# Modulation chunks 0 to 2 in four column groups a step, chunk 3 summed by VectorE during the down projections of a hybrid transformer block

## The chip, the cores and the metric

The kernel runs on one core of a Trainium2 chip. The metric is the device time of one execution in microseconds; the time before is the median of 3 runs.

## The reference

One block of a diffusion transformer works on 256 latent tokens and 256 context tokens of width 2048. A vector `c` gives a modulation of six chunks of 2048 numbers. Two of them (shift and scale of the first norm) are needed for latents and context, the other four for the latents alone: the gate of the mixer, shift and scale of the second norm, the gate of the feed-forward network. In the kernel these four are the chunks 0, 1, 2 and 3.

```python
m_lat = jnp.split((jax.nn.silu(c) @ ada_w[i] + ada_b[i])[:, None, :], N_MOD, axis=-1)
...
a_lat = _modulate(h_lat, norm1_g[i], m_lat[0], m_lat[1]) @ w_in[i]
...
mix_l = jnp.concatenate([hyena_l, _retention_out(r_l, g_l),
                         _s5_out(y5_l, u_l, ...)], axis=-1) @ w_out[i]
...
h_lat = h_lat + m_lat[2] * mix_l
h_lat = h_lat + m_lat[5] * _conv_ffn(_modulate(h_lat, norm2_g[i], m_lat[3], m_lat[4]), ...)
...
return _rmsnorm(h_lat, norm_f)
```

The mixer has three parts: a Hyena convolution by Fourier transforms, a retention of 8 heads with decays in both directions, and an S5 state space scan. The feed-forward network is an up projection to twice 5632 features, a 3 by 3 convolution of one half, a gelu, the product with the other half and a down projection to 2048.

## The kernel before

Features lie on partitions, tokens along the free dimension. All weights come from HBM in blocks of 256 rows by 512 columns (512 KB). `split_w` loads a block by SP's DMA queue into a page of the ring "raw", ScalarE casts it to the high part (L454), VectorE takes the difference as the low part (L456), and `prod` makes three products of each pair (high by high, high by low, low by high: L461 to L463). `feat_block` has 24 products of 256 columns for one block. The products sum in two of the four PSUM banks "mm" per group of 512 features; small work uses three banks "sm", the modulation one bank "ad".

The large products follow each other: the S5 input while norm 1's modulation arrives, the keys, the values in two halves, the gate in two halves and the queries, the three Hyena projections, the output projection, then the feed-forward network in six groups of up and down projections. Between their blocks, tasks emit a piece of other work: the S5 chain, the retention, the Hyena chain, and `t_ada`, the modulation of chunks 0 to 3. A task's rate says how many of its steps are emitted per block: `RK` and `RV` in the keys and values, `RG` in gate and queries, `RH` in the Hyena projections, `RW` in the output projection, `RF` in the up projections. A scheduler of the language then puts each engine's instructions in order by their priority (the order of emission, with the weights' loads and casts moved ahead) and by the times at which it reckons that they can start. On the chip each engine takes its instructions in that order.

A chunk of the modulation is a vector of 2048 times a matrix of 2048 by 2048. `ada_matmul` makes it on TensorE, with 32 columns as weights (`cs`) and the matrix moving, 128 rows a step. The 2048 columns are four quarters `q` of 512, and quarter `q` is written to PSUM partitions 32q to 32q + 31, a column group of its own. A step is half of that, one page of 512 KB with two quarters:

```python
raw = [load_a(I["ada25"][c, kt, half]) for half in range(2)]
for half in (1, 0):
    for e in range(2):
        ...
    if (kt, half) != (KT - 1, 0):
        yield
```

The operands are 32-bit, and the trace has two records for each of these products. `ada_vector` instead adds each page, times its row's element of `cs`, to a page on VectorE (L428, L430), and sums over partitions by products with ones (L435). `ADV` lists the chunks that go this way: 1 and 2. `ada_store` transposes the sums (L397) into `ada_cols`. Pages come from the ring "ada", whose size after the S5 input is the first number of `RN`.

In `down`, each group's sums go straight to the residual, four instructions of 256 elements per 512 features (L1419):

```python
V.scalar_tensor_tensor(h_of(mt), at(m), ada_cols[:, 3, mt:mt + 1], h_of(mt), ALU.mult, ALU.add)
```

So chunk 3 is needed at the first down projection. In `retention`, the scores of the two heads of a pair are made one head after the other (L1158), each followed by its own decay and product with the values.

Of the kernel before, what the change touches and what calls it, by code (L numbers as in the profile page):

```python
# [16 lines left out]
P = 128  # L17
# [39 lines left out]
def _lay(i):  # L57
    """The inputs as the kernel reads them: slices, transposes and constants of the shapes."""
# [84 lines left out]
    # constants of the shapes  # L143
# [24 lines left out]
RN=[2,3,3,3];SA=40000;SF=30000;R0=10;R1=1;R2=1;RS=4;RK=2;RV=3;RG=.8;RH=.8;RW=.75;RF=.8;RT=1.2;RR=3;RY=.75;PR=500;ADV=[1,2];ORD=[0,1,2,3];RP=1.5;RQ=20;KS=5;PW=800;AR=[6,8,8,8,7,5,5,5];ZE=[1,3];VE=[0,1,3];UE=[1,3]  # L168
class _Pages:
    """Tags of fixed sizes in the slot pool, taken and given back in the order of the program."""  # L170
# [12 lines left out]
class _Ring:  # L183
    """Tags taken in turn."""
# [9 lines left out]
class _Task:  # L194
    """Work that is emitted piece by piece between the blocks of the large products."""
# [23 lines left out]
def tile_dit(ctx: ExitStack, tc: tile.TileContext, I, out: bass.AP, dbg=None):  # L219
# [14 lines left out]
    @contextmanager  # L234
    def stream(name, start):
        """Instructions whose order of priority starts at -start and goes on from use to use."""
        n = counts.get(name, 0)
        with tc.high_priority(offset=tc.cur_priority + start - n):
            before = tc.cur_priority
            yield  # L240
            counts[name] = n + tc.cur_priority - before
# [4 lines left out]
    def resize(kind, n):  # L246
        """A ring of n pages of 4 KB."""
        tags = ring[kind].tags
        while len(tags) < n:
            tags.append(pages.take(4))  # L250
        while len(tags) > n:
            pages.give(tags.pop())
# [53 lines left out]
    def sum_squares(ps, sq, first, last):  # L306
        """Sums over the partitions and parts of sq [P, n, w], a token on each partition."""
# [6 lines left out]
    def inv_rms(ps, n, w):  # L314
        """1/sqrt(sum/n + eps) of w tokens' sums, on all partitions."""
# [76 lines left out]
    def ada_store(c, ps):  # L392
        """Four rows of 512 columns to their places."""
# [10 lines left out]
    def ada_matmul(c):  # L404
        """2048 of the modulation's columns for the latents, as products of TensorE."""
        ps = ada_bank()
        for kt in range(KT):
            raw = [load_a(I["ada25"][c, kt, half]) for half in range(2)]
            for half in (1, 0):
                for e in range(2):  # L410
                    q = 2 * half + e
                    T.matmul(ps[32 * q:32 * q + 32, :], cs[:, kt, :], raw[half][:, e, :],  # L412
                             start=(kt == 0), stop=(kt == KT - 1), skip_group_check=True)
                if (kt, half) != (KT - 1, 0):
                    yield
# [3 lines left out]
    def ada_vector(c):  # L419
        """The same, summed over the rows' tiles by VectorE and over partitions by TensorE."""  # L420
        ps = ada_bank()
        for half in range(2):
            tag = pages.take(4)
            acc = slot(tag, [P, 2, 512])
            for kt in range(KT):
# [5 lines left out]
                if kt < KT - 1:  # L431
                    yield
            for e in range(2):
# [4 lines left out]
            if half == 0:  # L438
                yield
# [3 lines left out]
    def ada25():  # L443
        """The other four chunks of the modulation (2048 columns each), for the latents."""
# [14 lines left out]
    def prod(ps, a, b, first, last):  # L459
        """ps += a.T @ b with a = (high, low), b = (high, low)."""  # L460
# [12 lines left out]
    def feat_block(src, k0, at, mv, first, last):  # L473
        """256 rows of the weights into 512 features' sums: a bank's first start clears it for both."""
# [15 lines left out]
    hyk = [dram.tile([P, 4, 512], F32, name=f"hyk{o}") for o in range(2)]  # L490

    def sin_reduced(out_ap, x, w, k):
        """sin of x (SBUF [n, w]) with the argument reduced to [-pi, pi]; x is overwritten."""
# [8 lines left out]
    def hyena_filters():  # L502
# [36 lines left out]
        for o in range(2):  # L539
            # even and odd parts of the filter's lags  # L540
# [31 lines left out]
            for ft in (2, 3, 0, 1):  # L572
# [7 lines left out]
                if ft == 2:  # L580
                    # the first row is frequency 256, of the even part
# [10 lines left out]
    s5l = const.tile([P, 4, 2, 32], F32, name="s5l")  # L592
    s5 = {}
    # real parts and -/+ imaginary parts of lambda_bar to the powers 4, 8, 16 and one more
# [29 lines left out]
    def s5_prepare():  # L624
# [33 lines left out]
        # (lambda_bar - 1) / lambda  # L658
# [16 lines left out]
        # block-diagonal output matrices for the products within a chunk  # L675
# [3 lines left out]
        for qt in range(4):  # L679
            # the powers of lambda_bar times the input matrix  # L680
# [42 lines left out]
            # the products within a chunk by distance, then as a matrix of tokens by tokens  # L723
# [28 lines left out]
    # ======================= norm 1 and the S5 input, as the modulation arrives =======================  # L752
# [84 lines left out]
    # ======================= S5 =======================  # L837
# [3 lines left out]
    def s5_scan_input(v, quarter, held):  # L841
        """The chunks' additions to the states: of the context into v, of the latents into held."""
# [15 lines left out]
    def s5_add(v, dst, src, step, n, k):  # L858
        """v at dst, dst + step .. += lambda_bar^(4 * 2^k) * v at src, src + step .., n of them."""
# [23 lines left out]
    def s5_sum(v):  # L883
        """The state after 64 chunks from nothing, at 63."""
# [6 lines left out]
    def s5_scan(v):  # L891
        """From the state at 0 and the chunks' additions at 1..63, the states before all chunks."""
# [38 lines left out]
    def s5_chain():  # L931
# [26 lines left out]
        for hb in range(2):  # L958
# [21 lines left out]
            # in channels by tokens, where the context's part of u4 was  # L980
# [34 lines left out]
    # ======================= retention: keys and values =======================  # L1015
# [459 lines left out]
```

## Time and profile before

| | |
|---|---|
| median of 3 runs | 1506.35 us (1502.78 to 1508.24) |
| profiled execution, span from first to last instruction | 1506.4 us |
| TensorE busy (products) | 1459.1 us, 97% |
| VectorE busy | 1040.6 us, 69% |
| ScalarE busy | 658.0 us, 44% |
| DMA engines' time in packets | 65.4% of the span |
| read from HBM | 312.62 MB |

The profile is of one execution, of its own time: its span, 1506.4 us, lies between the lowest and the highest of the runs, and no other time of it is given. PE is TensorE, PEld its weight loads, DVE VectorE, ACT ScalarE, SP the engine whose queue starts the DMA transfers. A busy PE is not a PE at its peak, as its products overlap in the pipeline; distances between the starts of products are the better measure.

### The profile page before, as it was taken

To read this page: it belongs to the slowest core of one execution; us is meant where nothing else is said; L and a number is where in the kernel's file an instruction comes from. 1 tells how busy PE (TensorE), PEld (TensorE's weight loads), DVE (VectorE), ACT (ScalarE), POOL (GpSimd) and SP (SyncE) were. 2 spreads that over 40 slices of the span, in tenths; PEclk is the share of its full clock that TensorE was granted. 3 is DMA by queue.
4 is the path that set the end of the run, shared out by engine and by line. 5 is a ranking of instruction groups with operands and counts; after the bars stand their busy time and mean duration, and the time that the engine had idled before them with its cause. 6 is when DMAs were issued, how large, how long until landed. Compare 5 with 4: busy or idle time off the path is not lost.

```text
span 1506.4 us, 27320 instructions
## 1 busy us (share of the span) xinstructions
PE 1459.1 (97%) x11180; PEld 1314.7 (87%) x11180; DVE 1040.6 (69%) x1772; ACT 658.0 (44%) x974; POOL 10.9 (1%) x9
## 2 busy tenths in 40 slices
PE   6998999999999999999999999999999999999997
PEld 3566687678888987788899999999999999999997
DVE  6579519897869887653777665775667577657756
ACT  6337741213576433232554443443444344434434
POOL 0000000000000000000000000000000000000000
PEclk9999999999999999999999999999999999999998
DMA  9788635568877887677465666556665666656562
GB/s 352 260 313 291 229 101 197 183 194 278 281 252 253 299 303 261 219 226 251 145 182 183 185 182 184 185 177 192 183 183 182 182 183 183 185 183 184 178 189 90
DMA packets 89956, 318.58 MB, mean 211 GB/s; under 512 B 12039, under 2 KB 12584, under 8 KB 89384
## 3 DMA queue, kind: packets, MB, share of 16 engines
q1 hardware_dynamic: 89832, 316.85, 65.4%
q8 instruction: 87, 1.43, 0.4%
q14 instruction: 37, 0.30, 0.1%
HBM read 312.62 MB, written 4.19 MB: 210 GB/s over the span
## 4 chain that ended last, share of the span: by engine, by line
PE 83%; DVE 7%; DMA 5%; ACT 3%; issue 1%; SPq 0%; DVEq 0%; ACTq 0%
PE mm L461 24%; PE mm L462 23%; PE mm L463 23%; DMA s4k<-in_ada_dram 4%; PE ad L412 4%; DVE s4k L456 1%; DVE s4k L430 1%; PE sm L852 1%; PE ad L373 1%; PE sm L576 1%; PE mm L339 1%; PE sm L546 1%; DMA s4k<-in_x_t_dram 1%; PE sm L1158 0%; PE sm L1164 0%
## 5 line engine op out<-in xcount | busy, mean ns | idle before, releaser
L456 DVE TENSOR_TENSOR s4k<-s4k,s4k 128x1024 fp32r<-128x1024 f32 x376 | 459.6, 1223 | 324.1 <-ACT s4k L454 300.5
L454 ACT CAST s4k<-s4k 128x1024 fp32r<-128x1024 f32 x376 | 393.8, 1048 | 654.7 <-PE mm L462 483.3
L462 PE MATMUL mm<-s4k,s4k 128*128 128x256 f32 (+1 forms) x2144 | 629.0, 294 | 1.5 <-DVE s4k L775 1.2
L461 PE MATMUL mm<-s4k,s4k 128*128 128x256 f32 (+1 forms) x2144 | 626.9, 295 | 3.5 <-ACT s4k L454 3.1
L463 PE MATMUL mm<-s4k,s4k 128*128 128x256 f32 (+1 forms) x2144 | 624.7, 294 | 3.2 <-DVE s4k L456 3.2
L461 PEld LDWEIGHTS mm<-s4k,s4k 128*128 128x128 f32 x2144 | 411.9, 193 | 27.3 <-issue 12.9
L462 PEld LDWEIGHTS mm<-s4k,s4k 128*128 128x128 f32 x2144 | 414.3, 193 | 18.4 <-issue 8.2
L463 PEld LDWEIGHTS mm<-s4k,s4k 128*128 128x128 f32 x2144 | 412.1, 193 | 17.2 <-issue 6.9
L461 PE MATMUL mm<-s8k,s4k 128*128 128x256 f32 x960 | 272.7, 285 | 0.0
L462 PE MATMUL mm<-s8k,s4k 128*128 128x256 f32 x960 | 271.7, 284 | 0.0
L463 PE MATMUL mm<-s8k,s4k 128*128 128x256 f32 x960 | 271.1, 284 | 0.0
L461 PEld LDWEIGHTS mm<-s8k,s4k 128*128 128x128 f32 x960 | 183.9, 192 | 14.4 <-issue 12.6
L463 PEld LDWEIGHTS mm<-s8k,s4k 128*128 128x128 f32 x960 | 183.7, 192 | 4.3 <-issue 3.4
L462 PEld LDWEIGHTS mm<-s8k,s4k 128*128 128x128 f32 x960 | 184.3, 192 | 2.7 <-issue 2.5
L1396 DVE SCALAR_TENSOR_TENSOR t<-mm,s4k,t 128x189 f32<-128x189 f32 (+2 forms) x352 | 131.9, 424 | 7.9 <-ACT t L1388 6.3
L430 DVE SCALAR_TENSOR_TENSOR s4k<-s4k,cs,s4k 128x1024 f32<-128x1024 f32 x60 | 76.8, 1280 | 21.0 <-DMA s4k<-in_ada_dram 20.4
L412 PE MATMUL ad<-s4k,cs 128*32 128x512 f32 x256 | 62.7, 612 | 1.0 <-DMA s4k<-in_ada_dram 1.0
L1419 DVE SCALAR_TENSOR_TENSOR s4k<-mm,ada_cols,s4k 128x256 f32<-128x256 f32 x96 | 39.9, 477 | 4.7 <-PE mm L463 4.7
L373 PE MATMUL ad<-s4k,cs 128*32 128x256 f32 x512 | 35.6, 392 | 4.7 <-DMA s4k<-in_ada_dram 4.0
L1388 ACT ACTIVATE t<-mm,s4k 128x256 f32<-128x256 f32 x44 | 24.7, 562 | 14.6 <-PE mm L463 13.6
L466 ACT CAST s8k<-t 128x512 fp32r<-128x512 f32 x38 | 23.0, 616 | 18.2 <-DVE t L1403 9.3
L373 PEld LDWEIGHTS ad<-s4k,cs 128*32 128x32 f32 x512 | 13.8, 110 | 19.1 <-DMA s4k<-in_ada_dram 5.7
(281 smaller groups left out, 1023.5 us busy)
## 6 DMA issues: line engine op xcount, KB each, us to landing
s4k<-in_ada_dram SPq DMA_DIRECT2D x192, 512.0 KB, 4.9
s4k<-in_w_up_dram SPq DMA_DIRECT2D x176, 512.0 KB, 3.7
s4k<-in_w_down_dram SPq DMA_DIRECT2D x88, 512.0 KB, 3.7
s4k<-in_w_in_dram SPq DMA_DIRECT2D x80, 512.0 KB, 4.9
s4k<-in_w_out_dram SPq DMA_DIRECT2D x32, 512.0 KB, 4.6
s4k<-in_x_t_dram SPq DMA_DIRECT2D x8, 512.0 KB, 6.6
s4k<-in_ctx_t_dram SPq DMA_DIRECT2D x4, 512.0 KB, 10.2
hyk<-s8k SPq DMA_DIRECT2D x4, 512.0 KB, 4.0
```

The costliest lines, as they stand in the source:

```text
L373: T.matmul(ps[32 * q:32 * q + 32, :], cs[:, 2 * k2 + e, :], raw[:, e, 256 * part:256 * part + 256], start=(k2 == 0), stop=(k2 == 7), skip_ ...
L412: T.matmul(ps[32 * q:32 * q + 32, :], cs[:, kt, :], raw[half][:, e, :], start=(kt == 0), stop=(kt == KT - 1), skip_group_check=True)
L430: V.scalar_tensor_tensor(acc, raw, cs[:, kt, 0:1], acc, ALU.mult, ALU.add)
L454: S.copy(h, raw)
L456: V.tensor_tensor(lo, raw, h.bitcast(F32), ALU.subtract)
L461: T.matmul(ps, a[0], b[0], start=first, stop=False, skip_group_check=True)
L462: T.matmul(ps, a[0], b[1], start=False, stop=False, skip_group_check=True)
L463: T.matmul(ps, a[1], b[0], start=False, stop=last, skip_group_check=True)
L466: S.copy(h, src)
L1388: S.activation(acc[:, e, :], at(m), AF.Identity, bias=cw[:, 9, mt:mt + 1], scale=cw[:, 4, mt:mt + 1])
L1396: V.scalar_tensor_tensor(dst[:, r0:r1, c0:c1], src[:, r0 + dy:r1 + dy, c0 + dx:c1 + dx], cw[:, tap, mt:mt + 1], dst[:, r0:r1, c0:c1], ALU. ...
L1419: V.scalar_tensor_tensor(h_of(mt), at(m), ada_cols[:, 3, mt:mt + 1], h_of(mt), ALU.mult, ALU.add)
```

## The change

Chunks 0, 1 and 2 are made by `ada_matmul`, and a step of it now loads both pages of 128 rows and makes all four quarters. Chunk 3 is made by `ada_vector`, with two empty steps between the last addition and the products with ones. The rates of the task are lower, as a step of `ada_matmul` is twice as large; no step is emitted in the up projections (`RF=0`), and the down projections emit some at a new rate `RD`. The ring "ada" has 3 pages at first and 2 from the gate projections on.

The down projections of the groups 0 to 4 no longer add to the residual. Their sums are collected in two new pages `dsum`: copied by ScalarE for group 0, added by VectorE from PSUM, 512 elements an instruction, for the others. Before the last down projection the task is finished, and `gated` adds the collected sums times the gate to the residual. The last group is added to the residual as before. In `retention` the scores of both heads of a pair are made first, in turns, into two banks. Comments and docstrings are emptied as well.

```diff
-RN=[2,3,3,3];...RK=2;RV=3;RG=.8;RH=.8;RW=.75;RF=.8;...ADV=[1,2];...
+RN=[3,3,3,3];...RK=.5;RV=.5;RG=.5;RH=.5;RW=.5;RF=0;RD=.45;...ADV=[3];...
...
     def ada_matmul(c):
         ps = ada_bank()
         for kt in range(KT):
             raw = [load_a(I["ada25"][c, kt, half]) for half in range(2)]
-            for half in (1, 0):
-                for e in range(2):
-                    q = 2 * half + e
-                    T.matmul(ps[32 * q:32 * q + 32, :], cs[:, kt, :], raw[half][:, e, :],
-                             start=(kt == 0), stop=(kt == KT - 1), skip_group_check=True)
-                if (kt, half) != (KT - 1, 0):
-                    yield
+            for q in range(4):
+                T.matmul(ps[32 * q:32 * q + 32, :], cs[:, kt, :], raw[q // 2][:, q % 2, :],
+                         start=(kt == 0), stop=(kt == KT - 1), skip_group_check=True)
+            if kt < KT - 1:
+                yield
...
                 if kt < KT - 1:
                     yield
+            yield
+            yield
             for e in range(2):
                 q = 2 * half + e
                 T.matmul(ps[32 * q:32 * q + 32, :], ones[:, 0:1].to_broadcast([P, 32]), acc[:, e, :],
                          start=True, stop=True, skip_group_check=True)
             pages.give(tag)
-            if half == 0:
-                yield
...
+    resize("ada", 2)
     tag_sg = pages.take(8)
...
     def retention():
         for pr in range(4):
             yb = sm_bank()
+            pss = [sm_bank(), sm_bank()]
+            for s in range(2):
+                for e in range(2):
+                    ph = slice(64 * e, 64 * e + 64)
+                    T.matmul(pss[e][:, L * s:L * s + L], k_t[ph, pr, 128 * s:128 * s + 128], q_t[ph, pr, :],
+                             start=True, stop=True)
             for e in range(2):
                 hd = 2 * pr + e
-                ph = slice(64 * e, 64 * e + 64)
-                ps = sm_bank()
-                for s in range(2):
-                    T.matmul(ps[:, L * s:L * s + L], k_t[ph, pr, 128 * s:128 * s + 128], q_t[ph, pr, :],
-                             start=True, stop=True)
+                ps = pss[e]
...
+    dsum = [slot(pages.take(8), [P, 8, L]) for _ in range(2)]
...
+    def with_down():
+        t_ada.run(RD)
+
+    def gated(cg):
+        for mt in range(4 * cg, 4 * cg + 4):
+            V.scalar_tensor_tensor(h_of(mt), dsum[cg // 2][:, mt % 8, :], ada_cols[:, 3, mt:mt + 1], h_of(mt),
+                                   ALU.mult, ALU.add)
...
-            bk, at = gemm_feat(I["w_down"], cg, mv, lambda: None, kcs)
+            bk, at = gemm_feat(I["w_down"], cg, mv, with_down, kcs)
+            if finish is None:
+                for pr in range(2):
+                    k0 = 4 * (cg % 2) + 2 * pr
+                    acc = dsum[cg // 2][:, k0:k0 + 2, :].rearrange("p m n -> p (m n)")
+                    if g == 0:
+                        S.copy(acc, bk[pr])
+                    else:
+                        V.tensor_tensor(acc, acc, bk[pr], ALU.add)
+                continue
...
         else:
+            if n == len(groups) - 1:
+                t_ada.finish()
+                for cg in range(4):
+                    gated(cg)
             sums = down(n, last_squares if n == len(groups) - 1 else None)
```

## Rows read from the trace of the kernel before

**Rows 1.** The page, busy time of each engine, its share and instructions.

```profile
PE 1459.1 (97%) x11180; PEld 1314.7 (87%) x11180; DVE 1040.6 (69%) x1772; ACT 658.0 (44%) x974; POOL 10.9 (1%) x9
```

**Rows 2.** Windows: us, busy us (count) by engine, PEclk, DMA share, GB/s.

```profile
160.00:200.00 40.00, 36.26 (x258) 29.14 (x258) 20.68 (x52) 29.57 (x73) 0.00 (x0) 0.91 0.56 187
200.00:326.00 126.00, 126.00 (x655) 88.69 (x654) 96.66 (x196) 31.92 (x54) 0.00 (x0) 1.00 0.53 168
326.00:430.00 104.00, 97.86 (x681) 90.73 (x679) 87.62 (x128) 43.42 (x77) 7.19 (x4) 0.98 0.83 279
430.00:470.00 40.00, 35.35 (x248) 32.55 (x247) 27.07 (x47) 38.01 (x66) 0.00 (x0) 0.96 0.72 237
...
735.00:1480.00 745.00, 745.00 (x6211) 745.00 (x6209) 507.72 (x756) 325.31 (x362) 0.00 (x0) 1.00 0.60 181
...
1448.00:1470.00 22.00, 22.00 (x186) 22.00 (x185) 12.05 (x15) 7.58 (x8) 0.00 (x0) 1.00 0.61 188
1470.00:1494.00 24.00, 23.88 (x201) 23.79 (x199) 16.57 (x29) 15.72 (x27) 0.00 (x0) 1.00 0.16 44
```

**Rows 3.** Groups by line and shape: xcount | busy, mean ns | idle, releasers.

```profile
L430 DVE SCALAR_TENSOR_TENSOR s4k<-s4k,cs,s4k 128x1024 f32<-128x1024 f32 x60 | 76.8, 1280 | 21.0 <-DMA s4k<-in_ada_dram 20.4
...
L412 PE MATMUL ad<-s4k,cs 128*32 128x512 f32 x256 | 62.7, 612 | 1.0 <-DMA s4k<-in_ada_dram 1.0
...
L1419 DVE SCALAR_TENSOR_TENSOR s4k<-mm,ada_cols,s4k 128x256 f32<-128x256 f32 x96 | 39.9, 477 | 4.7 <-PE mm L463 4.7
...
L1403 DVE TENSOR_TENSOR t<-t,mm 128x512 f32<-128x512 f32 x22 | 14.9, 678 | 0.0
...
L435 PE MATMUL ad<-s4k,ones 128*32 128x512 f32 x16 | 4.2, 603 | 1.1 <-DVE s4k L430 1.1
```

**Rows 4.** Timeline of TensorE near 299 us: start, us, instruction.

```profile
298.71 0.39 PE L463 MATMUL mm<-s4k,s4k 128*128 128x512 f32 x1
298.93 0.39 PE L461 MATMUL mm<-s4k,s4k 128*128 128x512 f32 x1
299.25 1.05 PE L412 MATMUL ad<-s4k,cs 128*32 128x512 f32 x4
300.24 0.50 PE L462 MATMUL mm<-s4k,s4k 128*128 128x512 f32 x1
300.57 0.39 PE L463 MATMUL mm<-s4k,s4k 128*128 128x512 f32 x1
```

**Rows 5.** Timeline of TensorE near 223 us.

```profile
223.28 1.07 PE L412 MATMUL ad<-s4k,cs 128*32 128x512 f32 x8
224.27 0.39 PE L461 MATMUL mm<-s4k,s4k 128*128 128x256 f32 x1
```

**Rows 6.** TensorE's waits, 326 to 470 us: us, times, longest.

```profile
PE mm L461 <- ACT s4k L454: 3.1, 2, 2.8
PE mm L463 <- DVE s4k L456: 3.0, 3, 2.1
...
PE ad L435 <- DVE s4k L430: 1.1, 1, 1.1
```

**Rows 7.** Timeline of TensorE ahead of the feed-forward network.

```profile
721.11 1.05 PE L412 MATMUL ad<-s4k,cs 128*32 128x512 f32 x4
...
726.62 1.05 PE L412 MATMUL ad<-s4k,cs 128*32 128x512 f32 x4 [0.21 <-DMA s4k<-in_ada_dram]
...
728.50 1.06 PE L397 MATMUL ad<-ident,s4k 128*128 128x128 f32 x4
```

**Rows 8.** Timeline of TensorE at a head's scores.

```profile
483.00 1.13 PE L1158 MATMUL sm<-s4k,s4k 64*128 64x256 f32 x4
484.05 0.39 PE L463 MATMUL mm<-s4k,s4k 128*128 128x256 f32 x1
```

**Rows 9.** Timeline of VectorE in the feed-forward network.

```profile
1200.12 1.22 DVE L456 TENSOR_TENSOR s4k<-s4k,s4k 128x1024 fp32r<-128x1024 f32 x1 [1.66 <-ACT s4k L454]
1203.00 1.23 DVE L456 TENSOR_TENSOR s4k<-s4k,s4k 128x1024 fp32r<-128x1024 f32 x1 [1.66 <-ACT s4k L454]
```

More of the change, by code (lines that the diff above doesn't have):

```diff
@@ L165, in _lay @@
     return o
-RN=[2,3,3,3];SA=40000;SF=30000;R0=10;R1=1;R2=1;RS=4;RK=2;RV=3;RG=.8;RH=.8;RW=.75;RF=.8;RT=1.2;RR=3;RY=.75;PR=500;ADV=[1,2];ORD=[0,1,2,3];RP=1.5;RQ=20;KS=5;PW=800;AR=[6,8,8,8,7,5,5,5];ZE=[1,3];VE=[0,1,3];UE=[1,3]
+RN=[3,3,3,3];SA=40000;SF=30000;R0=10;R1=1;R2=1;RS=4;RK=.5;RV=.5;RG=.5;RH=.5;RW=.5;RF=0;RD=.45;RT=1.2;RR=3;RY=.75;PR=500;ADV=[3];ORD=[0,1,2,3];RP=1.5;RQ=20;KS=5;PW=800;AR=[6,8,8,8,7,5,5,5];ZE=[1,3];VE=[0,1,3];UE=[1,3]
 class _Pages:
```

## The prediction

> **What bounds the kernel now.** I read the busy shares of the page first: TensorE works 97% of the span, VectorE 69%, ScalarE 44% [rows 1]. A share over the whole span hides stages, so next came busy time by stage [rows 2]. In the feed-forward network (735 to 1480 us) TensorE is busy all the time at full clock: nothing on another engine is late there, and only TensorE work that goes away could shorten it. From 200 to 326 us it is the same, while chunk 0 of the modulation runs on TensorE. The one stage that differs is 326 to 470 us, where chunk 1 and then chunk 2 are summed by VectorE: TensorE is idle for 104 - 97.86 = 6.1 us and 40 - 35.35 = 4.7 us, and its granted clock of 0.98 and 0.96 costs another 2.1 and 1.6 us. So 14.5 us are lost there. The groups of instructions by line give the prices [rows 3], the timeline shows what a modulation step costs between two products of a weight block [rows 4, 5], the waits say who was late in that stage [rows 6].
>
> The kernel is thus bound by TensorE's instruction stream. An edit counts by the TensorE time that it takes out, and by the few waits that it ends or adds.
>
> **The change, part by part.**
>
> *Chunks 0 to 2 in four column groups.* A half step of before, two products of two passes each (x4 in the trace), begins at 299.25 and the next product at 300.24: 0.99 us. The product ahead of it holds TensorE for 0.32 us where its neighbour took 0.22, and the one behind for 0.33, so going in and out costs about 0.19 more: 1.18 us a set [rows 4]. At 223.28 two half steps happen to stand side by side, and the eight passes together also take 0.99 us until the next product [rows 5]. So four column groups run at the price of two, and the new loop makes that the rule. Before: 62.7 us busy [rows 3] at 1.05 a set [rows 4] are 59.7 sets (64 half steps, a few of them paired by chance). After: 3 chunks of 16 steps are 48 sets. 11.7 sets fewer, 1.18 each: -13.8 us. Three of the old sets, though, are the last of chunk 3, in the wait for norm 2 (the third of them at 726.62), where the products have nothing else to do [rows 7]; taking them away saves nothing: +3.5.
>
> *Chunk 3 by VectorE, one chunk fewer there.* Per chunk VectorE needs two sets of products with ones. Four such sets are 4.2 us busy in before [rows 3], two remain: -2 x 1.18 = -2.4 us. The four transposes of chunk 3's store, 1.06 us, stood in the wait for norm 2 [rows 7] and now stand among the products of a down projection: +1.1.
>
> *What VectorE does in the down projections.* The rates give 52 steps up to the end of the output projection: 48 for chunks 0 to 2, 4 of chunk 3's 35. The other 31 at 0.45 a block take 69 of the 88 blocks, so chunk 3 ends in the fifth of the six down projections' blocks. Each adds one instruction of 1.28 us [rows 3] about every 6 us. The evictions get cheaper: four of 0.477 us for 512 features (1.9 us) become two of 0.678 (1.4), or ScalarE copies in the first group [rows 3]. VectorE is at 508 of 745 us there [rows 2]. Its cast waits for ScalarE's, and has 1.66 us idle ahead of it in each block of 2.88 us [rows 9]; the rings hold four pages of cast weights, so a cast that is late by less than some blocks holds up no product. I cost this at nothing. Without that cover it would be 32 x 1.28 = 41 us less the evictions' saving of some 13. DMA adds 0.45 load to each weight load there: 181 x 1.45 = 262 GB/s, under the 279 that the chip moved from 326 to 430 us [rows 2]. SP's queue is in order, so a modulation load that waited for its page would hold up weights behind it; with two pages and a step every two blocks the page has been free for some us.
>
> *The gates at the end.* 16 instructions of 0.477 us [rows 3], 7.6 us, before the last down projection. They can run as soon as chunk 3 and the group before are done, while VectorE is busy 12.05 of 22 us before the last group and 16.57 of 24 in it [rows 2]. I take nothing; if they stood in front of everything, 7.6.
>
> *Retention's scores.* The two heads of a pair alternate, on partitions 0 to 63 and 64 to 127. Before, a head's products take from 483.00 to 484.05, 1.05 us [rows 8]; with 8 heads 8.4 us. If two heads run beside each other, 4.2 us go; if not, nothing. No row shows row groups side by side; the nearest is the set of four column groups, which overlapped fully [rows 5]. I take three quarters: -3.2. The Trainium skill (TensorE: Matmul & The Clock Gate, Part 3 on packing small matmuls) says that products in different row groups run concurrently in the same array. By it this term would be the whole 4.2; no row here shows it.
>
> *Waits that end.* From 326 to 470 us, the products' waits for the casts (3.1 and 3.0) and for the vector sums (1.1) are 7.2 us [rows 6]. All 76.8 us of vector sums leave that stage and the one behind it; they themselves waited 20.4 us for loads, with VectorE's casts queued behind them [rows 3]. Bounds: nothing, and all 14.5 us. I take half, which is about the waits named: -7.
>
> *Waits that begin.* A step now needs two pages at once, and from the gate projections on the ring has only two, so both loads of a step go out after the step before. TensorE waited 1.0 us in all for such loads in before [rows 3]. Twice that: +2. The upper bound is the rival below. Chunks 0 to 2 are due in time: gate 0 after 16 steps, chunk 2 after 48, that is in block 24 of 32 of the output projection.
>
> *The stage from 160 to 200 us* gets another page and fewer modulation steps; it has 3.7 us idle and 3.6 lost to the clock [rows 2]. I take nothing; up to 7 could go.
>
> Sum, against the profiled span of 1506.4 (the median of the runs, 1506.35, is the same): 1506.4 - 13.8 + 3.5 - 2.4 + 1.1 - 3.2 - 7 + 2 = 1486.6, say 1487.
>
> **The rivals.**
>
> *All waits go.* VectorE has room from 326 us on, TensorE gets modulation steps as filler, no low clock: 1506.4 - 13.8 + 3.5 - 2.4 + 1.1 - 4.2 - 14.5 = 1476, or 1469 with the stage at 160. For it: VectorE was full, 87.62 busy of 104 us [rows 2]. Against it: ScalarE is busy 38.01 of 40 us from 430 on with retention's decays and the weight casts, and that is not touched; the wait of 3.1 is for ScalarE [rows 6].
>
> *The saving slips away.* The products that are saved lie in the key and value projections, 200 to 326 us, where VectorE is at 96.66 of 126 us with the scans of the state space [rows 2]. If the scans set the pace of what follows, a shorter projection ends in a longer wait: the 24 sets now put into the later stages (28 us) come on top there, and only the sets of ones and the scores count. Some 1506.4 - 2.4 - 3 = 1501. Against it: VectorE had 29 us left there, and loses its 76.8 us of vector sums right behind [rows 3].
>
> *TensorE inherits VectorE's waits.* VectorE waited 20.4 us for 60 loads, 0.34 each [rows 3]. TensorE needs two loads a step: 0.68 x 48 = 32.6 us, and what is behind a waiting step in TensorE's queue, all products, waits too. Then 1506.4 - 13.8 + 3.5 - 2.4 + 1.1 + 32.6 = 1527. It outweighs the saving of 11.6 from 0.24 us a step on. Against it: chunk 3 ran on TensorE with two pages too, up to 727 us [rows 7], and all of TensorE's modulation steps waited 1.0 us [rows 3], since one step per two blocks leaves some 6 us for loads. The Trainium skill (TensorE: Matmul & The Clock Gate, Part 3) states that matmuls start and end in strict program order. That speaks for this rival's mechanism: no product could pass a step whose load is late.
>
> **How the numbers follow.** The sum as it stands (1478 to 1497): 0.64. All waits go (1469 to 1478): 0.14. The saving slips away (about 1500): 0.12. Inherited waits (1510 to 1527): 0.10. 1487 is the likeliest. From 1471 to 1503 it leaves out the last case, and a little of the second and third. A difference under 0.5% (7.5 us) can't be told from none: faster is below 1499, which the first two cases and a few hundredths of the third are, 0.80; the third and part of the fourth are the same, 0.12; slower 0.08.
>
> **What would show it.** Right: the modulation's products come as x8 sets of some 1.05 us, about 48 of them, busy near 50 us; a pair's score products come as x8 in about 1.1 us; no vector sums before the output projection's end, then 30 long ones among the down projections, with TensorE still busy all the time; idle time between 300 and 450 us down from 10.8 to about 5. Wrong: waits of TensorE for the modulation's loads over some us in all, idle time or a clock under 1.00 in the feed-forward stage, a longer last down projection, or a stage between 320 and 470 us whose idle time grew by what the projections before it lost.

## The result: 3.3% slower, and the profile after

The changed kernel takes 1554.49 us (median of 4 runs, 1554.2 to 1558.09) against 1505.91 us for the kernel before (median of 4, 1502.78 to 1508.24). The ratio is 1.0326, its 95% interval 1.0309 to 1.0343. The forecast was 1487 us, faster, with a range of 1471 to 1503: both the direction and the range were wrong. The profiled execution has a span of 1552.8 us, 46.4 more than that of before.

The page first: busy time of each engine, and the granted clock in 40 slices of the span.

```profile
PE 1482.8 (95%) x11300; PEld 1320.3 (85%) x11300; DVE 1001.5 (64%) x1708; ACT 664.7 (43%) x984; POOL 10.9 (1%) x9
...
PEclk9999999999999999999788999999999999999998
```

TensorE did not get less work but 23.7 us more [rows 1], and its share of the span fell, so it also stood still more. Near the middle of the span the clock drops for three slices. Groups by line, shapes kept apart (count | busy us, mean ns | idle us before them and what ended it):

```profile
L410 PE MATMUL ad<-s4k,cs 128*32 128x512 f32 x384 | 85.2, 604 | 1.5 <-DMA s4k<-in_ada_dram 1.5
...
L428 DVE SCALAR_TENSOR_TENSOR s4k<-s4k,cs,s4k 128x1024 f32<-128x1024 f32 x30 | 38.4, 1281 | 13.7 <-DMA s4k<-in_ada_dram 13.4
...
L1434 DVE TENSOR_TENSOR s8k<-s8k,mm 128x512 f32<-128x512 f32 x32 | 22.0, 688 | 0.5
...
L435 PE MATMUL ad<-s4k,ones 128*32 128x512 f32 x8 | 3.0, 833 | 13.0 <-DVE s4k L428 13.0
```

The modulation's products are 85.2 us busy, where about 50 were forecast and 62.7 were there before [rows 3]. A timeline of TensorE (start us, duration us, instruction) near the end of chunk 2 says why:

```profile
689.57 0.28 PE L461 MATMUL mm<-s8k,s4k 128*128 128x256 f32 x1
689.77 1.05 PE L410 MATMUL ad<-s4k,cs 128*32 128x512 f32 x4
690.76 0.38 PE L459 MATMUL mm<-s8k,s4k 128*128 128x256 f32 x1
...
691.66 1.05 PE L410 MATMUL ad<-s4k,cs 128*32 128x512 f32 x4
692.65 0.39 PE L459 MATMUL mm<-s8k,s4k 128*128 128x256 f32 x1
```

That is one step of the new loop, and it comes as two sets of x4 with six products of a weight block between them: each half costs 0.99 us to the next product, as much as all eight passes side by side [rows 5]. Counted over the trace, the 48 steps make 78 separate sets: 54 of x4, 13 of x8, 3 of x12 and 8 of x2 or x6.

The second surprise is where chunk 3 is summed. The instructions of its line, with their first and last start, and who waited for them:

```profile
L428 DVE SCALAR_TENSOR_TENSOR s4k<-s4k,cs,s4k x30: 1274/1283/1285, 716.3 to 816.2; 128x1024 f32<-128x1024 f32 x30
...
  PEld ad L435: 13.2, 1
  PE ad L435: 13.0, 1
```

All 30 additions run from 716.3 to 816.2 us, around norm 2 and in the first up projection. The first block of the down projections is fetched only at 898.9 us, as the line of SP's fetches shows:

```profile
L450 SPq DMA_DIRECT2D s4k<-in_w_down_dram x88: 327/328/328, 898.9 to 1519.3; - x88
```

TensorE's waits from 720 to 900 us (total us, times, longest) are now these:

```profile
PE ad L435 <- DVE s4k L428: 13.0, 1, 13.0
PE sm L311 <- DVE s4k L1322: 9.2, 1, 9.2
PE mm L459 <- ACT s4k L1356: 3.1, 1, 3.1
PE mm L460 <- DVE s4k L1357: 1.8, 1, 1.8
```

In the kernel before, the largest entry of the same view is 0.6 us in two waits:

```profile
PE ad L412 <- DMA s4k<-in_ada_dram: 0.6, 2, 0.4
```

VectorE's timeline shows what stands behind the wait of 9.2 us, a square of norm 2 (L1322) between two additions, and another addition that waits for its load:

```profile
739.19 1.27 DVE L428 SCALAR_TENSOR_TENSOR s4k<-s4k,cs,s4k 128x1024 f32<-128x1024 f32 x1
740.38 0.68 DVE L1322 TENSOR_TENSOR s4k<-s4k,t 128x512 f32<-128x512 f32 x1
740.99 1.27 DVE L428 SCALAR_TENSOR_TENSOR s4k<-s4k,cs,s4k 128x1024 f32<-128x1024 f32 x1
744.95 1.28 DVE L428 SCALAR_TENSOR_TENSOR s4k<-s4k,cs,s4k 128x1024 f32<-128x1024 f32 x1 [2.69 <-DMA s4k<-in_ada_dram]
```

On TensorE, the norm's sums and, later, chunk 3's products with ones start only after these:

```profile
741.12 1.86 PE L311 MATMUL sm<-ones,s4k 128*128 128x2 f32 x8 [9.22 <-DVE s4k L1322]
...
817.56 1.92 PE L435 MATMUL ad<-s4k,ones 128*32 128x512 f32 x4 [12.97 <-DVE s4k L428]
```

The same in windows (length; busy us of PE, PEld, DVE, ACT, POOL; granted clock; DMA share; GB/s):

```profile
200.00:326.00 126.00, 125.15 (x669) 100.83 (x667) 101.00 (x200) 33.51 (x56) 0.00 (x0) 1.00 0.39 127
326.00:430.00 104.00, 99.39 (x687) 82.56 (x686) 56.67 (x119) 70.37 (x131) 7.18 (x4) 0.98 0.55 181
430.00:470.00 40.00, 40.00 (x275) 29.68 (x273) 15.21 (x18) 13.11 (x15) 0.00 (x0) 1.00 0.82 267
740.00:830.00 90.00, 67.88 (x471) 63.70 (x472) 75.37 (x113) 32.28 (x47) 0.00 (x0) 0.78 0.71 234
830.00:1525.00 695.00, 695.00 (x5794) 695.00 (x5793) 462.64 (x655) 301.85 (x335) 0.00 (x0) 1.00 0.61 182
```

From 326 to 470 us TensorE now idles 4.6 us instead of 10.8 [rows 2], as forecast. From 740 to 830 us it idles 22 of 90 us at a granted clock of 0.78; before, that stretch was full at 1.00. From 830 us on nothing is lost.

To see where time goes between the traces, the start of the n-th of the 9456 weight products (the lines of `prod`) is compared. A product of the same number does the same work in both, up to the order of tasks.

```
product    before    after    after - before
    900     319.0    299.1       -19.9
   1500     443.2    443.9        +0.6
   2100     548.2    572.6       +24.4
   3000     703.0    717.3       +14.3
   3600     790.0    836.0       +46.0
   9300    1474.0   1520.0       +46.0
```

Most of the first 20 us gained is work put off: at product 900 the changed kernel has made 68 of its 384 passes of the modulation, which took TensorE 13 us, the kernel before 124 of its 256, in 27 us. By product 3000 chunks 0 to 2 are done in the changed kernel, and all but six sets of chunk 3 in the kernel before. Up to there the distances from start to start on TensorE sum to +24 us for the modulation's sets and the products with ones (80 against 56), -6 of idle time, -4 of low clock, and small terms. From product 3000 to 3600, 87 us become 119: +29 of idle time (30.2 against 1.2), +3 of low clock, +3 of small products, -3 of modulation.

### The profile page after: what moved, and what is told of

Read it like the earlier page. It is cut to its first block, busy times and chain, and to the rows that moved or that the text cites. A ratio compares the mean times of both kernels' runs of the same rounds, so it can differ in the third digit from the quotient of the medians.

```text
span 1552.8 us, 27485 instructions
## 1 busy us (share of the span) xinstructions
PE 1482.8 (95%) x11300; PEld 1320.3 (85%) x11300; DVE 1001.5 (64%) x1708; ACT 664.7 (43%) x984; POOL 10.9 (1%) x9
## 4 chain that ended last, share of the span: by engine, by line
PE 81%; DVE 8%; DMA 6%; ACT 3%; issue 2%; SPq 0%; DVEq 0%; ACTq 0%
PE mm L459 22%; PE mm L461 22%; PE mm L460 22%; DMA s4k<-in_ada_dram 4%; PE ad L410 4%; DVE s4k L454 2%; PE ad L373 1%; DVE s4k L428 1%; PE sm L574 1%; PE sm L971 1%; PE sm L850 1%; PE sm L544 1%; DVE s16k L866 1%; DVE t L864 1%; DMA s4k<-in_x_t_dram 1%
## 5 line engine op out<-in xcount | busy, mean ns | idle before, releaser
L459 PEld LDWEIGHTS mm<-s4k,s4k 128*128 128x128 f32 x2144 | 410.2, 192 | 42.7 <-issue 20.4
L459 PEld LDWEIGHTS mm<-s8k,s4k 128*128 128x128 f32 x960 | 184.0, 192 | 14.3 <-issue 12.6
L410 PE MATMUL ad<-s4k,cs 128*32 128x512 f32 x384 | 85.2, 604 | 1.5 <-DMA s4k<-in_ada_dram 1.5
L428 DVE SCALAR_TENSOR_TENSOR s4k<-s4k,cs,s4k 128x1024 f32<-128x1024 f32 x30 | 38.4, 1281 | 13.7 <-DMA s4k<-in_ada_dram 13.4
L1398 ACT ACTIVATE t<-mm,s4k 128x256 f32<-128x256 f32 x44 | 24.7, 562 | 20.4 <-PE mm L461 13.9
L373 PEld LDWEIGHTS ad<-s4k,cs 128*32 128x32 f32 x512 | 13.7, 110 | 21.5 <-DMA s4k<-in_ada_dram 7.4
L410 PEld LDWEIGHTS ad<-s4k,cs 128*32 128x32 f32 x384 | 12.2, 108 | 17.0 <-issue 5.8
```

What stands on the lines that cost most here:

```text
L373: T.matmul(ps[32 * q:32 * q + 32, :], cs[:, 2 * k2 + e, :], raw[:, e, 256 * part:256 * part + 256], start=(k2 == 0), stop=(k2 == 7), skip_ ...
L410: T.matmul(ps[32 * q:32 * q + 32, :], cs[:, kt, :], raw[q // 2][:, q % 2, :], start=(kt == 0), stop=(kt == KT - 1), skip_group_check=True)
L428: V.scalar_tensor_tensor(acc, raw, cs[:, kt, 0:1], acc, ALU.mult, ALU.add)
L459: T.matmul(ps, a[0], b[0], start=first, stop=False, skip_group_check=True)
L1398: S.activation(acc[:, e, :], at(m), AF.Identity, bias=cw[:, 9, mt:mt + 1], scale=cw[:, 4, mt:mt + 1])
```

## The experiments

Two theories share out the 46 us. **Split steps**: a step's two loads land one after the other, the order of TensorE's queue is made by when operands are reckoned to be there, and the halves are put where each is ready. **Early sums**: chunk 3's additions run as soon as a page of ring "ada" is free, ahead of the place at which they are emitted, and stand before norm 2 on VectorE. The rivals: that the split comes from the order of the four products in the step alone; that the loads, not VectorE's additions, make norm 2 late; and that chunk 3 among the down projections is a loss wherever it runs.

**e1: the products of a step in another order.** The late page's products go first, as in the kernel before.

```diff
-            for q in range(4):
+            for q in (2, 3, 0, 1):
```

> The changed kernel, with the four quarters of a modulation step in the order 2, 3, 0, 1, so that the first product needs the page that lands last. Theory: the steps of chunks 0 to 2 run as two half sets because the scheduler places the first two products as soon as the first page is there; the products of those chunks took 85.2 us of busy time where 48 whole sets would take about 50. Then x8 sets become the rule, their busy time falls to 50 to 58 us, and the time falls by 25 to 33 us, to 1521 to 1530. Rival: halves cost nothing by themselves, and the stages with the S5 and Hyena work are long because the modulation was moved into them: 1550 to 1556, whatever the sets look like.

1545.57 us, ratio 1.0257 (1.0222 to 1.0293); busy 73.8 us in 69 sets, 27 of them x8. All sets are whole up to 421 us and from 503 to 567 us; most are halves between these stretches and from 575 us on. The first 12 steps have a ring of three pages, the others two, and two pages alone don't split a step: 14 of those 36 steps are whole. What goes with it is the time since the step before began: 13 of the 14 whole steps come 9.2 us or more behind it, 18 of the 22 split ones 8.1 us or less. The order helps, but is not the whole cause: it takes away a third of the excess (11.4 of 35 us busy), and the expectation was missed by 15 us. It leaves what happens at norm 2 as it was (29.6 us idle from product 3000 to 3600).

**e2: chunk 3's pages from the weights' ring.** Nothing else is changed; an addition's page now comes in turn with the weight blocks' pages, so its load can't be issued long before the block beside which it is emitted.

```diff
-                raw = load_a(I["ada25"][c, kt, half])
+                raw = load_a(I["ada25"][c, kt, half], "raw")
```

> The changed kernel, with the pages of chunk 3's loads taken from the ring of the weights' pages instead of a ring of their own, so that a load can't run ahead of the weight blocks among which it is emitted. Theory: the loss of some 30 us at the start of the feed-forward network (idle time of TensorE 30.2 us between its products 3000 and 3600, and a low clock behind it) comes from the scheduler starting all of chunk 3's loads and vector sums as soon as a page is free, from 712 to 817 us, ahead of the squares of norm 2 and of the set of ones. Then the sums spread over the down projections, the idle time there falls to 2 us, and the time falls by 26 to 33 us to 1521 to 1529. Rival: vector sums cost the feed-forward network the same wherever they are, and three pages of weights with loads in between are too few for the down projections: 1545 or more, with idle TensorE among the down projections.

1525.37 us, ratio 1.0119 (1.0094 to 1.0143), as expected: 29 us less than the changed kernel. The additions and TensorE's longest wait from 720 to 900 us:

```profile
L428 DVE SCALAR_TENSOR_TENSOR s4k<-s4k,cs,s4k x30: 1277/1285/1287, 708.1 to 1426.0; 128x1024 f32<-128x1024 f32 x30
```

```profile
PE sm L311 <- DVE s4k L1322: 4.1, 1, 4.1
```

The additions are spread up to 1426 us, and the idle time from product 3000 to 3600 falls from 30.2 to 6.0 us. It was expected to fall to 2. Most of what is left is not the additions': e4 and e6 below, with none of them between 700 and 760 us, still idle 4.4 and 4.1 us there, in a wait that chunk 3's sets partly filled in the kernel before [rows 7]. In the feed-forward network TensorE takes 711.6 us from product 3600 on, against 707.7: four are lost, of which 2.9 are the sets of ones that now stand there.

**e3: both.**

> Both edits: order 2, 3, 0, 1 and chunk 3's pages from the weights' ring. Theory: the two losses are independent and the gains add: 1554 less 28 less 29, so 1490 to 1503, below the kernel before. Rival (one of the two only hides the other, as the time won ahead of the feed-forward network is lost at its start): 1520 or more.

1519.21 us, ratio 1.0083 (1.0053 to 1.0112); busy 72.9 us. The two nearly add up (9 and 29 apart, 35 together), and the expectation, 1490 to 1503, fails as e1's did: it took the sets to be whole.

**e7: without the loads of chunk 3.** Only the first page of each half is loaded, and added 16 times; the last gate is therefore another one.

```diff
-                raw = load_a(I["ada25"][c, kt, half])
+                if kt == 0:
+                    raw = load_a(I["ada25"][c, kt, half])
```

> The changed kernel, leaving out all loads of chunk 3 but the first of each half: VectorE adds the same page 16 times, so the gate of the feed-forward network is not the reference's. VectorE's instructions and their order stay. Theory: what was late at the start of the feed-forward network is the loads, with VectorE waiting in order for them (13.4 us of waits by its sums) and everything else of VectorE behind: idle time of TensorE there falls from 30 us to under 8, the time to 1522 to 1530. Rival: VectorE's own work is too much there (32 sums of 1.28 us beside casts and norm 2): idle time stays at 20 us or more, the time above 1540.

1539.86 us in one run; idle from product 3000 to 3600 is 20.8 us, where a cause in the loads alone would have left under 8. So the theory of the expectation fell; the idle time is the rival's, 20 us or more. With no load to wait for, the additions still stand before norm 2's squares, which TensorE now awaits 11.5 us:

```profile
PE sm L311 <- DVE s4k L1323: 11.5, 1, 11.5
```

**e8: the loads whole, the additions short.** Each addition takes 64 of 512 columns; the last gate is again another one.

```diff
-                    V.scalar_tensor_tensor(acc, raw, cs[:, kt, 0:1], acc, ALU.mult, ALU.add)
+                    V.scalar_tensor_tensor(acc[:, :, :64], raw[:, :, :64], cs[:, kt, 0:1], acc[:, :, :64], ALU.mult, ALU.add)
```

> The changed kernel, with chunk 3's vector sums cut to 64 of 512 columns, so that the gate of the feed-forward network is not the reference's; its loads stay whole. It is the counterpart of the run without loads, which kept 20.8 us of idle time at the start of the feed-forward network where the change has 30.2. Theory as that run left it: VectorE's own time there and the waits for loads each hold up norm 2's squares and the set of ones. Then short sums leave the waits for loads: idle time 12 to 25 us there, time 1530 to 1548. Rival (VectorE's time alone decides): idle time under 8 us, 1520 to 1528.

1522.72 us in one run, inside the rival's range and below the theory's. The additions and what VectorE waited for, then TensorE's longest wait from 720 to 900 us:

```profile
L428 DVE SCALAR_TENSOR_TENSOR s4k<-s4k,cs,s4k x30: 343/350/354, 714.4 to 807.3; 128x128 f32<-128x128 f32 x30
...
  DMA s4k<-in_ada_dram: 19.2, 16
```

```profile
PE sm L311 <- DVE s4k L1322: 3.4, 1, 3.4
```

VectorE waited even longer for loads than in the changed kernel (19.2 us against 13.4), in the same place, and yet TensorE idles only 5.7 us. 30 x (1281 - 350) ns = 28 us less of VectorE's time took 24.5 us off TensorE's idle time. VectorE's own time at that place is the price; the waits for loads add to it only beside long additions (30.2 us idle with them, 20.8 without, in e7).

**e4: e3 with rates that leave more time per step.** Chunks 0 to 2 begin faster, where three pages are there, and go slower where two are.

```diff
-...;RK=.5;RV=.5;RG=.5;RH=.5;RW=.5;...
+...;RK=.75;RV=.75;RG=.4;RH=.4;RW=.37;...
```

> The kernel with both edits (order 2, 3, 0, 1; chunk 3 in the weights' ring), with more steps of chunks 0 to 2 in the key and value projections, where three pages are free and whole sets were seen, and fewer behind: 0.75 a block there, 0.4 in gate, queries and Hyena, 0.37 in the output projection. Theory: a set falls in halves when its turn on TensorE comes before both loads have landed (a step every two blocks, loads of 5 to 7 us in a ring of two pages); with more time between steps whole sets become the rule. Busy time of the chunks' products 72.9 us before the edit, then 55 to 62; time 1503 to 1511. Rival: halves come whenever two pages land one after the other, whatever the rate: 70 us or more, 1515 to 1521.

1506.46 us (median of 10), ratio 1.001 (0.9994 to 1.0027), as expected. Busy time and a set:

```profile
L410 PE MATMUL ad<-s4k,cs 128*32 128x512 f32 x384 | 61.9, 609 | 7.8 <-DMA s4k<-in_ada_dram 7.8
```

```profile
343.51 1.07 PE L410 MATMUL ad<-s4k,cs 128*32 128x512 f32 x8
344.51 0.50 PE L461 MATMUL mm<-s4k,s4k 128*128 128x512 f32 x1
```

39 of the 57 sets are x8: the 18 steps with three pages and 21 of the 30 with two, where e3 has 14 whole of 36. Of these 21, 20 begin 9.1 us or more behind the step before, of the nine split ones eight 9.3 us or less. So whole sets with two pages go with time between steps, as the theory has it; that this is the time in which both loads land is argued, not shown. TensorE pays for it with 7.8 us of waits for loads where the changed kernel had 1.5. Even so the three chunks cost about as much as two did before, and the kernel is no faster than before.

**e5 and e6: chunk 3 alone.** The kernel before, its steps, its two chunks on VectorE, its scores and `RW=RF=0`, with chunk 3 added up by VectorE in the down projections (`RD=.5`) and gated at the end. In e5 its pages come from ring "ada", in e6 from the weights' ring.

```diff
-raw = load_a(I["ada25"][c, kt, half])
+raw = load_a(I["ada25"][c, kt, half], "raw" if c == 3 else "ada")
```

> The kernel before, with one part of the change alone: chunk 3 by VectorE during the down projections (0.5 steps a block, none in the output projection), sums collected and gated at the end. Chunks 0 to 2 and the scores as before, chunk 3's loads in the ring of the modulation. Theory: TensorE loses the 32 half sets of chunk 3 (some 33 us of it between 576 and 727 us, 3 of them in a wait), and the scheduler still starts the vector sums as soon as it can, so that the start of the feed-forward network loses 25 to 33 us: 1500 to 1512. Rival (the loss there came with the other parts of the change): 1473 to 1485.

> The same, with chunk 3's loads in the ring of the weights' pages, so that they keep to their places among the weight blocks. Theory: the gain of the part of the change that moves chunk 3 off TensorE, without the loss at the start of the feed-forward network: 1506 less 33, plus 3 (filler in the wait for norm 2) and 3 for two more sets of ones and the transposes among the products: 1476 to 1486, below both kernels. Rival: 1500 or more, if the output projection is held up by something else than TensorE once chunk 3 is gone from it.

e5: 1505.52 us (median of 10), ratio 1.0002 (0.9981 to 1.0023), in the expected range, but not by the expected loss. e6: 1490.5 us (median of 4, 1486.13 to 1494.06), ratio 0.9891 (0.9852 to 0.993), faster than both kernels, though 4.5 us above the expected range. The line of all additions (chunks 1 to 3) in e5, then its window from 540 to 700 us:

```profile
L430 DVE SCALAR_TENSOR_TENSOR s4k<-s4k,cs,s4k x90: 1268/1284/1287, 329.3 to 707.7; 128x1024 f32<-128x1024 f32 x90
```

```profile
540.00:700.00 160.00, 141.41 (x1041) 133.10 (x1040) 132.61 (x165) 53.99 (x67) 0.00 (x0) 0.93 0.78 266
```

The same two of e6:

```profile
L430 DVE SCALAR_TENSOR_TENSOR s4k<-s4k,cs,s4k x90: 1273/1284/1289, 332.9 to 1399.3; 128x1024 f32<-128x1024 f32 x90
```

```profile
540.00:700.00 160.00, 154.67 (x1184) 148.45 (x1183) 112.23 (x153) 59.84 (x74) 0.00 (x0) 0.98 0.59 194
```

With a ring of their own, not one of chunk 3's additions waits for the down projections: all are done by 709 us. VectorE is busy 132.61 of 160 us, and the Hyena chain is late: from product 2100 to 3000 TensorE idles 18.6 us, 15.2 of them for the chain's casts on ScalarE, at a clock of 0.93 in the window. The loss was expected at the start of the feed-forward network, where e5 idles only 3.8 us: that the number came out was luck. One argument of a load keeps them in place, and 15 us are kept. So the third rival falls: chunk 3 among the down projections is a gain, if it runs there. e6 is 17.3 us ahead of before at product 3000 and 20.4 at 3600; the feed-forward network gives 6.4 back (713.5 against 707.1 us, for sets of ones, transposes and 2.0 us of waits, nearly all for one low part of a weight block on VectorE).

**e11: the order of the scores alone**, in the kernel before.

> The kernel before with the order of the scores alone. Theory: pairs mostly split; a difference of 0 to -2 us to before, not to be told from none. Rival: four pairs side by side, -4 us; or the second score bank held over the pair delays other small work that uses the same three banks: +3 us or more.

1507.52 us (median of 10), ratio 0.9995 (0.9976 to 1.0013): nothing that can be told from none, as expected. Where a pair's products do stand together, here in the changed kernel, the second head takes no time of its own:

```profile
469.28 1.14 PE L1156 MATMUL sm<-s4k,s4k 64*128 64x256 f32 x8
470.34 0.38 PE L461 MATMUL mm<-s4k,s4k 128*128 128x256 f32 x1
```

Eight passes take 1.06 us until the next product, as four did [rows 8]. But this is one of four pairs. The other six heads come as x4 at 1.06 each.

**e9, e10, e12: putting the good parts together.** e9 has e6's chunk 3, but chunk 0 in whole sets (e1's order, `RK=.7`, `RV=.66`, `RG=RH=1.5`); e10 adds the scores in turns; e12 takes chunk 2's pages from the weights' ring as well (`"raw" if c >= 2`, `RH=.7`, `RW=.6`).

> Chunk 0 on TensorE with all four quarters a step (order 2, 3, 0, 1; three pages in the key and value projections, 0.7 and 0.66 steps a block), chunks 1 and 2 on VectorE as before the change (1.5 steps a block from the gate projections on), chunk 3 on VectorE in the down projections with pages from the weights' ring. Theory: against the run with chunk 3 alone moved (1490.5 us), chunk 0's products go from 28.5 us busy in half sets to about 17 in 16 whole sets, and their ways in and out get fewer: 1476 to 1483. Rival: the key and value projections end sooner, and what follows (the S5 chain, VectorE's sums that now start later) takes it back, as it did in the changed kernel, where 20 us won by product 900 were gone at product 1500: 1487 to 1494.

> The same, with the change's order of the retention's scores as well. In the trace of the changed kernel one pair of heads ran as x8 in 1.06 us, the price of one head before, but three of four pairs fell apart into heads. Theory: the scheduler splits most pairs, so the difference to the run without it is 0 to -2 us. Rival: all pairs run side by side here, and 4 us go.

> The last kernel (chunk 0 in whole sets, scores in turns), with chunk 2's loads in the weights' ring as chunk 3's, and its sums spread over the Hyena projections (0.7 a block) and the output projection (0.6) instead of run at the scheduler's will behind chunk 1's. In the run without it, TensorE was idle for 14.3 us between its products 2100 and 3000, waiting for ScalarE and VectorE pieces of the Hyena chain that stood behind vector sums. Theory: what holds up others is that the sums are started as soon as a page is free; with pages that come in the weights' order the idle time there falls to 5 us or less, and the time to 1480 to 1489. Rival: three pages of the ring are too few for 1.6 loads a block there, the weights come late: 1495 or more, with TensorE idle for casts.

e9: 1498.35 us (median of 7), ratio 0.9938 (0.9912 to 0.9964). e10: 1496.08 (median of 4), 0.9908 (0.9879 to 0.9937). e12: 1497.01 (median of 4), 0.9937 (0.9915 to 0.9959). All are below the kernel before by more than their intervals, none is shown to beat e6, and e9 and e12 miss their theories (1476 to 1483, 1480 to 1489). e10 differs from e9 by less than the intervals, as expected. e9 has what the change wanted, 16 steps in 16 sets of x8, and 17.9 us for a chunk. But VectorE begins its chunks later, and its additions then meet the Hyena chain, as e9's waits of TensorE say:

```profile
PE sm L459 <- ACT s8k L464: 9.8, 2, 6.9
...
PE sm L459 <- DVE t L1228: 3.8, 3, 1.6
```

From product 2100 to 3000 e9 idles 16.5 us, e6 5.3. e12 moves chunk 2's additions and lowers that from 14.3 (e10) to 9.8, but idles 4 us more from product 900 to 2100, where retention's products wait 4.7 us for VectorE's decays. The time moves from one wait to another. I read VectorE's room before norm 2 as the limit of all three; no run shows that by itself.

## Why the prediction was wrong, point by point

**What bounds the kernel: right.** From 830 us on TensorE is busy in 695.00 of 695.00 us, and the idle time that was added lies where another engine was late for it. The rest of the loss is more work of its own and a lower clock.

**Four column groups: the rate is right, the step to "the rule" failed.** "So four column groups run at the price of two, and the new loop makes that the rule": the first half holds (1.00 us for x8 in e4), the second does not. The program's loop says in which order steps are emitted, not that four products stay together. The term of -13.8 came out as +22.5 busy: 78 sets, not 48. With the late page's products first and three pages all sets are whole (e1's first 12 steps, e9), and with two pages mostly those that begin later behind the step before (e1, e4); the reading that fits is that a step's two pages are then both there at its turn. The sign was in the trace of before: chunk 0's 32 half steps are emitted two or three at one place (`RK=2`, `RV=3`), yet they came as 26 sets, only six of them x8. I had read the pairs as chance without asking what kept the others apart. The count was off as well: before has 56 sets, not 59.7, so even 48 whole sets would have saved 8, some 9.4 us.

**Chunk 3 on VectorE: the step that failed most.** "The rates give 52 steps up to the end of the output projection ... Each adds one instruction of 1.28 us [rows 3] about every 6 us. ... I cost this at nothing." The count of rates gives the place of emission. It is not the place of execution: VectorE was given the additions as soon as a page was free, and with pages that come in the weights' turn they spread to 1426 us (e2). In the changed kernel they ran from 716.3 to 816.2 us, in the one stretch where norm 2 waits on VectorE and TensorE on norm 2. Price: 29 us (e2), of VectorE's time (e8). My bound without cover (41 less some 13, so 28) has the size of the loss by chance: it was worked out for the down projections, and its 13 us of cheaper evictions have no part in what happened at norm 2. I gave it no chance of its own, since I looked for cover only where the text of the kernel put the work. Where the additions do run in the down projections, costing them at nothing is borne out: e2 loses 4 us there, 2.9 of them for the products with ones. So is the +3.5 for the sets that had filled the wait for norm 2 (e4 and e6 idle some 3 us more there than before).

**Gates at the end and the evictions: right.** From product 3600 to the last one of TensorE 707.7 us against 707.1, and the additions from PSUM take 688 ns, priced at 678 [rows 3].

**Scores: the mechanism right, the size off.** Row groups do run beside each other, as the Trainium skill says (TensorE: Matmul & The Clock Gate, Part 3 on packing small matmuls), and the trace agrees: 1.06 us for eight passes. But only one pair of four stands together, which is worth 1.1 us by these lines instead of 3.2; e11 is too coarse to show it.

**Waits that end and begin: about right.** Idle time from 326 to 470 us fell from 10.8 to 4.6 (the prediction's signs say 300 to 450 for that 10.8; rows 2 have it for 326 to 470). The low clock from 160 to 200 us, taken at nothing, went as well: 1.00 against 0.91 in before. TensorE waited 1.5 us for the modulation's loads, not the 2 more that I took.

**The rivals.** TensorE inheriting VectorE's waits for loads (1527) fell, at 1.5 us: I take it that a late half is put behind other products in the queue before it can hold them up, and that this is why the steps split. The slower time that it named came from elsewhere. "The saving slips away" saw a part: 19.9 us ahead at product 900, level at 1500, as the rest of chunk 0 and the start of chunk 1 are paid there, where before had one such set. It put this down to scans that set the pace and a longer wait; TensorE's wait there got shorter, and the time went into more of its own work.

**The sum.** The forecast's sum adds up as written. Two small readings in it are off: the evictions' saving by rows 3 is 80 x 0.477 less 32 x 0.678, or 16.5 us, where it has some 13, and the products beside a set take 0.10 and 0.11 us more, 0.21 where it has 0.19 [rows 4]. Of the 66 us between forecast (-19.4) and trace (+46.4), the sets with those of ones are 33 (forecast -12.7, measured +20), and the start of the feed-forward network 35 (forecast 0; 29.0 idle, 2.9 low clock, 2.8 slower small products). Waits and clock ahead of it were 5 better than forecast, smaller terms make up the rest.

What stays open: that halves are placed by when their loads are reckoned to land is argued from e1 and e4. The scheduler's reckoning was not read out, and the number of pages and the time between steps were not varied one at a time, as e4 also moves six more steps to where the ring has three pages.

## What to carry to other kernels

A rate of emission places work only on an engine that is busy; on one with slack a list scheduler runs it as soon as its buffers are free, so look up where its free pages let it start, and what is urgent there. If work is to stay beside a stream, take its buffers from that stream's own ring: here one argument of a load was worth 29 us in the changed kernel and 15 in e5 against e6. And products that are cheap only side by side need operands that arrive together: count the sets in the trace (x4 or x8), not the steps in the loop.

## What the hardware showed that was not expected

A wait of TensorE cost more than itself. The stretch in which it waited 9.22 us (up to 741.12) and the one in which it waited 12.97 us (up to 817.56) each run into a stretch at the lower of the two levels of the granted clock (the 0.50 of these windows, 1.2 GHz), 23.9 and 20.5 us long:

```profile
735.40:759.30 23.90, 11.71 (x50) 11.04 (x51) 18.53 (x29) 4.88 (x12) 0.00 (x0) 0.50 0.72 220
807.10:827.60 20.50, 8.76 (x35) 6.63 (x36) 15.32 (x29) 5.36 (x8) 0.00 (x0) 0.50 0.37 134
```

The set of ones at 817.56 is drawn with 1.92 us where a half step at 689.77 has 1.05. From product 3000 to 3600 the weight products lost about 5 us by it, against about 2 in before.
